# Bias pieces among the gates, paired groups at each new operand set, and x1 added by GpSimd, in a transformer block on one core

## The chip, the core and the metric

The kernel runs on one core of a Trainium2 chip. The core has five engines, each with its own instruction queue that is worked through in order: TensorE (PE, matrix products, weight loads shown apart as PEld), VectorE (DVE), ScalarE (ACT), GpSimd (POOL) and SyncE (SP, which here only issues transfers). 16 DMA engines move data; transfers that SP issues are on queue q1, those that GpSimd issues on q0. The metric is the device time of one execution in microseconds, as the median of several runs.

## The reference, cut to what matters

One block over x of shape (1, 2048, 1024), float32:

```
h      = rms_norm(x, norm1_g);   proj = h @ w_in          # 4608 columns: u, v | q, k, v | gates
y_a    = u * (w_s . layer_norm(v) + b_s)                  # gelu(u, v); chunks of 128 tokens
y_b    = neighbourhood_attention_2d(q, k, v, q_g, k_g, rpb)   # scores + bias from na_rpb, softmax
gates  = sigmoid(gate_pre + b_gate)
merged = gates[:, :D] * (y_a @ w_o_a) + gates[:, D:] * (y_b @ w_o_b)
x      = x + merged @ w_out                               # x1
h2     = rms_norm(x, norm2_g)
x      = x + square(relu(h2 @ w_ff1)) @ w_ff2             # up: 1024 -> 4096, down: 4096 -> 1024
```

## The kernel before, in words

Everything is computed transposed: features on the 128 partitions, tokens along the row, in two halves of 1024 tokens (h 0 and 1). Each float32 operand is split in a high and a low part (ACT casts the high part, DVE subtracts to get the low one), and a product is the sum of high x high, high x low and low x high.

The large products (the features of w_in, up and down) run in **groups**: a block of 256 output features by 1024 tokens, as seven products of half-sized operand sums in place of eight, in the order 1, 5, 6, 3, 7, 2, 4. A product is 12 matmuls of 128x128 by 128x512 for 4 operands (`seven`, matmul at L1537). It accumulates in a PSUM bank called z, x or y; after each product DVE or ACT **evacuates** the bank, that is adds or copies it to a tile in SBUF, and products that go on in the same bank wait for that. The stages of the program, with their start in the profiled execution: gates of half 0; the u features of half 1 (two groups, 243.8 us); gates of half 1 (eight groups, 278.0); values (450.5); keys and queries (to 880); attention; merge and output projection; then up of half 0 (16 groups, 1445.6), down of half 0 (1767.8), up of half 1 (2087.8) and down of half 1 (2408.2).

The operands of a product:

- `w_seven` (L1446): weights. SP loads two w_r tiles (L1458), GpSimd makes the sums w_s (L1464 to L1471), and `hilo` splits them (ACT cast L1418, DVE subtraction r_lo and t_lo L1422).
- `x_seven` (L1486): activations x_r and x_t, whose sums are made before and lie in DRAM (xf, hf, af). SP loads (L1497), ACT casts (L1505), DVE subtracts (L1509).
- `first_w` gives the values' and keys' weights their sums on GpSimd (L391 to L401, tiles w and t).

An up group (L1763 on) evacuates with a squared ReLU into tiles a_A to a_D, makes sums of them on GpSimd and stores them as af (L1816). **Down** (L1830 on) visits four output blocks j in turn, several times each, as af comes in: a visit is one group over up to four k. All seven evacuations of a visit are DVE additions to tile x1 (L1854), which is first loaded with the residual x1 from DRAM (L1439); the last visit's result is stored.

**Bias pieces.** Attention reads its biases from tables tb in DRAM. `bias_tables` (L1009 to L1077) makes them on GpSimd: memsets, a few loads with waits between (tbi L1021, sk L1024, tbx L1041), sums, and then 93 transfers tb<-tbi and tb<-tbx (L1056), all in one chain of 108 stages.

What sets the order: the kernel doesn't run its code in written order. `Plan` collects **steps** (one for each product) and **chains** of **stages** (a load, a cast, a subtraction, a sum, a store), each with an engine, a cost, a lead (how long before its first step it is due) and the buffers it takes and gives (51 buffers of one size). `Plan.run` then walks through the steps with planned times, and issues a stage behind a step if its engine is free in the plan and buffers are there, or when it is due; `put_off` can postpone one that is due. The result is only an order of instructions for each engine; on the chip an instruction starts when the engine reaches it and what it waits for has come.

Of the kernel before, what the change touches and what calls it, by code (L numbers as in the profile page):

```python
# [87 lines left out]
class Plan:  # L88
# [25 lines left out]
    def run(self):  # L114
# [156 lines left out]
class Block:  # L271
# [74 lines left out]
    def feat(self, h, xs, c0, row, act, dst, done, leads=(22, 14, 9)):  # L346
# [24 lines left out]
        ids = self.seven(w, xs, {1: copy(0, 0, True), 5: copy(1, 1, True), 6: copy(0, 1, False), 3: add(0, 1), 7: add(1, 1),  # L371
                                 2: add(0, 0), 4: (lambda bank: fin(1, 0, bank), 0, {"DVE": 0.7, "ACT": 0.7}, 0)})
        for i, p in ((0, 2), (1, 4)):
            def out(i=i):
                nc.sync.dma_start(dst(i), e[i][1].rearrange("p b t -> p (b t)"))
                self.give(e[i][0])
            done(i, (self.post(ids[p], [self.store(out, 1, 0)], 8), 1))
# [630 lines left out]
    def bias_tables(self, start, end):  # L1008
# [66 lines left out]
        c = self.plan.chain([Stage("POOL", 2.0, f, t, gv, 5 + 2.2 * (n - i), 0.0) for i, (f, t, gv) in enumerate(fs)], start=start)  # L1075
# [3 lines left out]
    def first_steps(self):  # L1079
# [31 lines left out]
        for c in range(2):  # L1111
            if c == 1:
                self.constants()
            self.first_w(0, 2 + c, len(plan.steps) + 6)

            def act(i, v):
                nc.scalar.activation(v, v, AF.Gelu)
            self.feat(1, xs, C_U + c * 256, lambda b: self.rows["in", 1, b], act,
                      lambda i, c=c: self.ut[(2 * c + i) * P : (2 * c + i + 1) * P, 1024:2048],
                      lambda i, d: self.ut_done[1].append(d))  # L1120
        for c in range(8):
# [3 lines left out]
            gates(1, xs, c)  # L1125
        start = len(plan.steps)
# [353 lines left out]
    def x_seven(self, src, after):  # L1480
# [4 lines left out]
        for name, (p0, p1) in self.X_PART.items():  # L1485
# [21 lines left out]
            def sub(name=name):  # L1507
# [4 lines left out]
                [Stage("SP", self.DMA * n / 2, load, 1, 0, 11, 3.0),  # L1512
                 Stage("ACT", 0.1 + 0.48 * n, cast, n - 1, 0, 6, 0.3), Stage("DVE", 0.1 + 0.58 * n, sub, 0, 0, 3, 0.2)],
# [3 lines left out]
    def seven(self, w, xs, evac, mid=None):  # L1517
# [4 lines left out]
        banks = {}  # L1522
        ids = {}
        for p in (1, 5, 6, 3, 7, 2, 4):
            bank = {5: "x", 3: "x", 2: "y"}.get(p, "z")
            (wn, wi), (xn, xi) = self.W_AT[p], self.X_AT[p]

            def mm(p=p, bank=bank, wn=wn, wi=wi, xn=xn, xi=xi):
                if p in (1, 5, 2):
                    banks[bank] = self.ps(bank, "mm" if p == 1 else "s")  # L1530
                out = banks[bank]
                at = lambda v, k: v[:, k] if wi is None else v[:, k, wi]
                for k in range(n):
                    a = [at(v, k) for v in w[0][wn][1]]
                    b = [v if xi is None else v[:, xi] for v in xs[k][0][xn][1]]
                    for j, (u, v) in enumerate(((0, 0), (0, 1), (1, 0))):
                        nc.tensor.matmul(out, a[u], b[v], start=(p in (1, 5, 2) and k == 0 and j == 0),  # L1537
                                         stop=(k == n - 1 and j == 2), skip_group_check=p in (6, 3, 7, 4))

            fn, take, costs, free = evac[p]  # L1540
            ids[p] = plan.step(3 * n * self.MM, mm, [w[1][wn]] + [x[1].get((xn, xi), x[1][xn]) for x in xs],
                               (lambda fn=fn, bank=bank: fn(banks[bank])), take, costs, free, ids.get({6: 1, 3: 5, 7: 6, 4: 7}.get(p)))
        w[2].first = ids[1]
# [74 lines left out]
    def out_proj(self, h, mgs):  # L1618
# [5 lines left out]
        for c in range(4):  # L1624
# [67 lines left out]
            def out(part, x, i, c=c):  # L1692
# [10 lines left out]
                ((k1, 1), (k2, 1)), start=step, due=24)  # L1703
# [60 lines left out]
    def up(self, h, mid):  # L1764
# [3 lines left out]
        xs = [self.x_seven(self.hf[h, c], (self.hf_done[h, c],)) for c in range(4)]  # L1768
        for c in range(self.NU):
            w = self.w_seven(w1, [0, 2, 4, 6], [1, 3, 5, 7], c * 256)  # L1770
            e = {}
# [24 lines left out]
            ids = self.seven(w, xs, mk())  # L1796
# [29 lines left out]
            if c in mid:  # L1826
                for f in mid[c]:
                    f()

# [102 lines left out]
```

## Time and profile before

| | us |
|---|---|
| median of 3 runs | 2734.75 |
| lowest and highest run | 2733.2, 2739.95 |
| the profiled execution, device time | 2740.49 |
| its span on the core | 2738.7 |
| PE busy (granted clock 0.967 on the mean) | 2553.1 |
| DVE, ACT, POOL busy | 1810.2, 1181.1, 1103.9 |

The profile is one execution. Its page gives busy times by engine; the other views give the same trace by stretch (busy time of each engine, the clock that TensorE was granted as a share of full speed, the DMA engines' busy share), by queue, by line, as a chain of what released what, and as lists of what an engine waited for. An engine's idle time matters only where the next matmul waits for it.

### The profile page before, as it was taken

The numbers are of one execution on the slowest core, as the hardware profiler recorded it, in microseconds if no ns is written. First come the engines' busy times: TensorE is split into PE (matmuls) and PEld (weight loads), VectorE is DVE, ScalarE is ACT, GpSimd is POOL, SyncE is SP. The second block draws the span as 40 slices with busy tenths as digits, with TensorE's granted clock in tenths as the row PEclk, the third lists the DMA queues.
The fourth block names the chain that finished last, engine by engine and source line by source line (L and its number), as shares of the span: only waits on it lengthen the run. The fifth ranks groups of instructions, "written<-read, shape, count | busy, mean of one in ns | idle before, by whom it ended". The sixth has DMA issues, their size and how long they took to land.

```text
span 2738.7 us, 34122 instructions
## 1 busy us (share of the span) xinstructions
PE 2553.1 (93%) x11832; PEld 2074.2 (76%) x11832; DVE 1810.2 (66%) x2588; ACT 1181.1 (43%) x1857; POOL 1103.9 (40%) x852
## 2 busy tenths in 40 slices
PE   7997999858898899999998999899998999979999
PEld 6776888647677777778886888778887888868887
DVE  5656657545888666563647566688777665677876
ACT  6555446334554555532324433433334343433341
POOL 3553541350000111132434677634343777743442
PEclk9998999979999999999999999999999999989999
DMA  5878658787768999996856444553436444374443
GB/s 169 288 222 263 212 186 287 187 214 219 238 179 210 295 309 310 322 365 231 277 197 199 143 146 156 203 202 135 169 131 228 153 157 154 137 273 140 149 148 112
DMA packets 401181, 569.20 MB, mean 208 GB/s; under 512 B 34093, under 2 KB 268756, under 8 KB 401008
## 3 DMA queue, kind: packets, MB, share of 16 engines
q1 hardware_dynamic: 388736, 553.45, 62.5%
q0 software_dynamic: 8128, 13.55, 2.1%
q8 instruction: 93, 1.52, 0.2%
q10 hardware_dynamic: 4144, 0.02, 0.1%
q14 instruction: 80, 0.66, 0.1%
HBM read 363.89 MB, written 202.98 MB: 207 GB/s over the span
## 4 chain that ended last, share of the span: by engine, by line
PE 69%; DMA 13%; DVE 9%; SPq 3%; ACT 2%; issue 2%; POOL 1%; ACTq 0%; DVEq 0%; POOLq 0%
PE z L1537 30%; PE x L1537 15%; PE fg L331 11%; PE y L1537 7%; DMA vw<-vs 2%; DMA x_t<-xf 2%; SPq L845 1%; PE z L713 1%; DMA x_r<-xf 1%; DVE x_r L1509 1%; PE fg L502 1%; PE pv L1292 1%; DMA y<-ya 1%; DMA bias<-tb 1%; PE x L713 1%
## 5 line engine op out<-in xcount | busy, mean ns | idle before, releaser
L1537 PE MATMUL z<-x_t,t_hi 128*128 128x512 f32 x1184 | 371.4, 395 | 32.5 <-DVE x L1854 25.8
L1464 POOL TENSOR_TENSOR w_s<-w_r 128x512 f32<-128x512 f32 (+3 forms) x87 | 150.3, 1727 | 524.4 <-DVE x L1854 226.3
L1422 DVE TENSOR_TENSOR r_lo<-w_r,r_hi 128x1024 fp32r<-128x1024 f32 (+3 forms) x174 | 254.2, 1463 | 83.1 <-ACT r_hi L1418 83.1
L1537 PEld LDWEIGHTS z<-x_t,t_hi 128*128 128x128 f32 x1184 | 224.2, 190 | 84.5 <-ACT t_hl L1418 16.8
L1167 POOL CAST q<-qn 128x256 fp32r<-128x256 f32 x128 | 49.3, 427 | 478.3 <-DMA qn<-qs 229.3
L1537 PE MATMUL z<-x_t,t_lo 128*128 128x512 f32 x592 | 233.9, 395 | 3.9 <-DVE t_lo L1422 3.9
L1537 PE MATMUL x<-x_r,t_hl 128*128 128x512 f32 x888 | 218.1, 393 | 8.1 <-DVE x_r L1509 5.8
L1418 ACT CAST r_hi<-w_r 128x1024 fp32r<-128x1024 f32 (+3 forms) x174 | 171.6, 988 | 119.5 <-PE z L1537 47.1
L1537 PEld LDWEIGHTS x<-x_r,t_hl 128*128 128x128 f32 x888 | 167.8, 189 | 45.6 <-DVE x_r L1509 7.5
L1505 ACT CAST x_r<-x_r 128x1024 fp32r<-128x1024 f32 x104 | 107.6, 1049 | 209.0 <-PE x L1537 152.2
L1537 PE MATMUL z<-x_r,r_hi 128*128 128x512 f32 x592 | 186.6, 397 | 5.5 <-DVE x_r L1509 5.5
L1537 PE MATMUL z<-x_t,r_hi 128*128 128x512 f32 x592 | 184.9, 394 | 5.9 <-DVE x L1854 3.4
L1537 PE MATMUL y<-x_r,r_hi 128*128 128x512 f32 x592 | 183.6, 391 | 0.0
L1537 PE MATMUL x<-x_r,r_hi 128*128 128x512 f32 x592 | 182.4, 389 | 0.0
L331 PE MATMUL fg<-y,w_hi 128*128 128x512 f32 x512 | 163.1, 400 | 7.9 <-DMA y<-ya 5.2
L1470 POOL TENSOR_TENSOR w_s<-w_r 128x512 f32<-128x512 f32 (+3 forms) x87 | 166.0, 1908 | 3.9
L1509 DVE TENSOR_TENSOR x_r<-x_r,x_r 128x1024 fp32r<-128x1024 f32 x104 | 147.4, 1436 | 20.7 <-ACT x_r L1505 20.7
L331 PE MATMUL fg<-mg,w_hi 128*128 128x512 f32 x512 | 157.7, 389 | 0.0
L1422 DVE TENSOR_TENSOR t_lo<-w_s,t_hi 128x1024 fp32r<-128x1024 f32 (+3 forms) x87 | 136.7, 1572 | 19.7 <-DMA af<-a_D 11.5
L1471 POOL TENSOR_TENSOR w_s<-w_r,w_s 128x512 f32<-128x512 f32 (+3 forms) x87 | 133.6, 1535 | 25.4 <-DVE t_lo L1422 7.8
L1854 DVE TENSOR_TENSOR x<-z,x 128x512 f32<-128x512 f32 x152 | 104.6, 688 | 59.2 <-PE z L1537 58.9
L1537 PEld LDWEIGHTS z<-x_r,r_hi 128*128 128x128 f32 x592 | 113.2, 192 | 29.6 <-DVE x_r L1509 5.8
(258 smaller groups left out, 5996.0 us busy)
## 6 DMA issues: line engine op xcount, KB each, us to landing
w_r<-in_w_ff_dram SPq DMA_DIRECT2D x116, 512.0 KB
x_r<-af SPq DMA_DIRECT2D x64, 512.0 KB
w_r<-in_w_in_dram SPq DMA_DIRECT2D x34, 512.0 KB
gt<-fe SPq DMA_DIRECT2D x32, 512.0 KB
x_r<-xf SPq DMA_DIRECT2D x32, 512.0 KB
qn<-qs SPq DMA_DIRECT2D x64, 256.0 KB
g<-gt SPq DMA_DIRECT2D x64, 256.0 KB
x<-x SPq DMA_DIRECT2D x32, 512.0 KB
```

The lines of the kernel that those rows point to most:

```text
L331: self.nc.tensor.matmul(out, w[p], x[q], start=(i == 0 and j == 0), stop=(i == n - 1 and j == 2))
L713: nc.tensor.matmul(out, a[u], b[v], start=(p in (1, 5, 2) and k == 0 and j == 0), stop=(k == 3 and j == 2), skip_group_check=p in (6, 3, 7 ...
L1167: nc.gpsimd.tensor_copy(e[0][1][:, cb].rearrange("p l (r c) -> p (l r) c", c=16), e[1][1].rearrange("p l (r f c) -> p f (l r) c", f=4, c=1 ...
L1418: nc.scalar.copy(e[name + "_"][1][0], e[name][1])
L1422: nc.vector.tensor_tensor(lo, e[name][1], hi.bitcast(F32), ALU.subtract)
L1464: nc.gpsimd.tensor_tensor(s23[:, :, 1], r1[:, :, 0], r1[:, :, 1], ALU.subtract)
L1470: nc.gpsimd.tensor_tensor(s23[:, :, 0], r1[:, :, 1], r1[:, :, 0], ALU.subtract)
L1471: nc.gpsimd.tensor_tensor(e["t4"][1], r2[:, :, 0], s23[:, :, 0], ALU.subtract)
L1505: nc.scalar.copy(hi, lo.bitcast(F32))
L1509: nc.vector.tensor_tensor(lo, lo.bitcast(F32), hi.bitcast(F32), ALU.subtract)
L1537: nc.tensor.matmul(out, a[u], b[v], start=(p in (1, 5, 2) and k == 0 and j == 0), stop=(k == n - 1 and j == 2), skip_group_check=p in (6, ...
L1854: nc.vector.tensor_tensor(v, bank, v, ALU.add)
```

## The change

1. The bias chain: its stages are planned on an engine of their own, "bias", with 3.7 us each (before: POOL, 2.0 us), and it may start before the u groups of half 1 (before: at the values). The instructions are still GpSimd's.
2. `feats` and `sevens`: groups can be run product by product together (1a 1b 5a 5b 6a 6b ...). This is done for the two u groups of half 1 (their constants' loads now come after them) and for groups 0 and 1 of each up, with shorter leads for the second group's weights and longer ones for x operands c = 1 to 3 (`early`).
3. Down: on the first visit of a block, products 1, 5, 6 and 4 are copied by ACT into a new tile "o", and 3, 7, 2 are added by DVE. x1 is loaded for later, and GpSimd adds it to the tile (128x1024) between two visits.
4. The planner: a stage with a lag (a store) is planned 2 us later and may be put off (`late`); a DVE or ACT stage may stand ahead of an evacuation if by the plan it ends 0.3 us and the evacuation's cost before the end of the next step (`room`). The hf sums' due time goes from 24 to 20.

```diff
-        self.lag = lag
+        self.lag, self.late = lag, 2.0 if eng == "SP" and lag else 0.0
...
+            t -= c.stages[k].late
-            if c.stages[k].eng not in ("ACT", "DVE") or i + 2 >= n or (c.first is not None and c.first <= i):
+            if (c.stages[k].eng not in ("ACT", "DVE") and not c.stages[k].late) or i + 2 >= n or (c.first is not None and c.first <= i):
...
+            room = self.steps[i + 1].cost - 0.3 if i + 1 < n else 0.0
-                    b = max(c.begin() if k else r, clock.get(st.eng, 0.0), now)
-                    if (b + st.cost > end + 0.1) if st.eng in ("DVE", "ACT") else b > end:
+                    b = max((c.begin() if k else r) + st.late, clock.get(st.eng, 0.0), now)
+                    if (b + st.cost > end + max(0.1, room - s.costs.get(st.eng, 0.0))) if st.eng in ("DVE", "ACT") else b > end:
...
-        c = self.plan.chain([Stage("POOL", 2.0, f, t, gv, 5 + 2.2 * (n - i), 0.0) for i, (f, t, gv) in enumerate(fs)], start=start)
+        c = self.plan.chain([Stage("bias", 3.7, f, t, gv, 8 + 3.9 * (n - i), 0.0) for i, (f, t, gv) in enumerate(fs)], start=start)
...
+        self.feats(xs, [first(0), first(1)])
+        self.constants()
...
-    def seven(self, w, xs, evac, mid=None):
+    def seven(self, w, xs, evac):
+        return self.sevens([(w, evac)], xs)[0]
+
+    def sevens(self, groups, xs):
...
+            for g, (w, evac) in enumerate(groups):
...
-                ((k1, 1), (k2, 1)), start=step, due=24)
+                ((k1, 1), (k2, 1)), start=step, due=20)
...
-        xs = [self.x_seven(self.hf[h, c], (self.hf_done[h, c],)) for c in range(4)]
+        xs = [self.x_seven(self.hf[h, c], (self.hf_done[h, c],), 1.3 * c) for c in range(4)]
...
+            w = self.w_seven(w1, [0, 2, 4, 6], [1, 3, 5, 7], c * 256, (16, 10, 6) if c == 1 else (22, 14, 9))
...
+        for cs in [(0, 1)] + [(c,) for c in range(2, self.NU)]:
...
-                    x1[m] = (e, plan.chain([self.load(e, "x1", [2, 512], self.x1[h, m], 5)], (self.x1_done[h, m],)))
...
+            new = j not in acc
+                    if first:
+                        e[m] = self.take([2, 512], F32, "o")
+                    nc.scalar.copy(e[m][1][:, b], bank)
+                return (f, int(first), {"ACT": 0.6}, 0)
...
+            put = copy if new else (lambda m, b, first: add(m, b))
-                             {1: add(0, 0), 5: add(1, 1), 6: add(0, 1), 3: add(0, 1), 7: add(1, 1), 2: add(0, 0), 4: add(1, 0)})
+                             {1: put(0, 0, True), 5: put(1, 1, True), 6: put(0, 1, False), 3: add(0, 1), 7: add(1, 1), 2: add(0, 0), 4: put(1, 0, False)})
...
+                            nc.gpsimd.tensor_tensor(e[m][1], e[m][1], x["x1"][1], ALU.add)
+                        ld = plan.chain([self.load(x, "x1", [2, 512], self.x1[h, i], 12)], (self.x1_done[h, i],))
+                        ch = plan.chain([Stage("POOL", 3.0, plus, 0, 1, 4, 0.3)], ((ld, 1),), start=ids[4])
```

The order of instructions shows the change at three places. (Lines of the changed file stand some 10 lower: L1056 is L1066, L1509 is L1520, L1854 is L1883.)

GpSimd, from the last gates to the bias tables, before: the last sums of the values' and keys' weights (tiles w and t), then the bias chain's first memset, its loads, and its pieces.

```order
L400 TENSOR_TENSOR t_3129<-w_3014 128x512
L401 TENSOR_TENSOR t_3152<-w_3055,t_3129 128x512
L1020 MEMSET tbi 120x96
L1021 DMA tbi<-in_na_rpb_dram 120x31
L1024 DMA sk<-tbi 1920x1x96
L1031 DMA tbi<-in_column_mask_dram 128x96
L1041 DMA tbx<-sk 16x15x32 x8
L1047 TENSOR_TENSOR tbx<-tbx,tbi 128x360
L1049 MEMSET tbi 128x528
L1050 COPY tbi<-tbx 128x192
L1056 DMA tb_83<-tbi 8x16x360
L1056 DMA tb_82<-tbx 8x16x192
```

GpSimd at the same place now, from a gate group's last weight sums (w_s) on:

```order
L1482 TENSOR_TENSOR w_s_3124<-w_r_3052,w_s_3077 128x512
L1066 DMA tb_82<-tbi 8x16x264
L1066 DMA tb_84<-tbi 8x16x288
L1066 DMA tb_83<-tbi 8x16x360
L401 TENSOR_TENSOR t_3202<-w_3083 128x512
L402 TENSOR_TENSOR w_3083<-w_3083,w_3103 128x512
L1066 DMA tb_82<-tbi 8x16x264
L410 TENSOR_TENSOR t_3202<-w_3083 128x512
L411 TENSOR_TENSOR t_3221<-w_3103,t_3202 128x512
L1066 DMA tb_84<-tbi 8x16x96
L1066 DMA tb_84<-tbx 8x16x192
L1066 DMA tb_83<-tbi 8x16x360
```

The chain's first memset now stands 71 rows above the last sum; its loads and 21 pieces are spread over the gates' sums, and the other 72 pieces follow that sum with no other GpSimd work between but the three instructions that make the second table's tbi.

SP where the first down begins, before: the af stores of up's 15th group (of 16), x1 loads (x<-x_95), operands x_t and x_r.

```order
L1816 DMA af<-a_A 128x1024
L1816 DMA af<-a_C 128x1024
L1816 DMA af<-a_B 128x1024
L1816 DMA af<-a_D 128x512
L1439 DMA x_14708<-x_95 128x1024
L1439 DMA x_14710<-x_95 128x1024
L1497 DMA x_t_14717<-af 128x1024
L1439 DMA x_14746<-x_95 128x1024
L1439 DMA x_14748<-x_95 128x1024
L1497 DMA x_r_14753<-af 128x1024
```

SP now, from 15 rows behind the 15th group's store of a_A on: the last stores of the 16th, operands, weights (w_r), and the first two x1 loads.

```order
L1835 DMA af<-a_B 128x1024
L1835 DMA af<-a_D 128x512
L1508 DMA x_t_14923<-af 128x512
L1508 DMA x_r_14936<-af 128x1024
L1508 DMA x_t_14952<-af 128x1024
L1508 DMA x_r_14968<-af 128x1024
L1469 DMA w_r_14984<-in_w_ff_dram 128x4x256
L1469 DMA w_r_14986<-in_w_ff_dram 128x4x256
L1508 DMA x_t_15006<-af 128x512
L1450 DMA x_15025<-x_95 128x1024
L1508 DMA x_t_15063<-af 128x1024
L1450 DMA x_15083<-x_95 128x1024
```

Before, the first x1 load stood 4 rows behind the 15th group's store of a_A, and the fourth 8; now the first stands 24 rows behind it, with eleven operands x_t and x_r and five weight tiles between, and the second two rows further.

DVE at the end of the first down, before: the last two visits' additions to x1 tiles, and the subtractions for the coming up (r_lo of a weight, x_r of its operands).

```order
L1854 TENSOR_TENSOR x_14748<-z,x_14748 128x512
L1854 TENSOR_TENSOR x_14874<-z,x_14874 128x512
L1854 TENSOR_TENSOR x_14876<-x,x_14876 128x512
L1422 TENSOR_TENSOR r_lo<-w_r_16823,r_hi 128x1024
L1509 TENSOR_TENSOR x_r_16945<-x_r_16945,x_r_16992 128x1024
L1509 TENSOR_TENSOR x_r_16929<-x_r_16929,x_r_16981 128x1024
L1509 TENSOR_TENSOR x_r_16912<-x_r_16912,x_r_16965 128x1024
L1509 TENSOR_TENSOR x_r_16914<-x_r_16914,x_r_16967 128x1024
L1854 TENSOR_TENSOR x_14874<-z,x_14874 128x512
L1854 TENSOR_TENSOR x_14874<-x,x_14874 128x512
L1854 TENSOR_TENSOR x_14876<-z,x_14876 128x512
```

The same now (tile o in place of x1's):

```order
L1883 TENSOR_TENSOR o<-y,o 128x512
L1520 TENSOR_TENSOR x_r_16929<-x_r_16929,x_r_16967 128x1024
L1883 TENSOR_TENSOR o<-z,o 128x512
L1520 TENSOR_TENSOR x_r_16961<-x_r_16961,x_r_17011 128x1024
L1883 TENSOR_TENSOR o<-z,o 128x512
L1883 TENSOR_TENSOR o<-x,o 128x512
L1433 TENSOR_TENSOR r_lo<-w_r_16839,r_hi 128x1024
L1520 TENSOR_TENSOR x_r_16980<-x_r_16980,x_r_17025 128x1024
L1883 TENSOR_TENSOR o<-z,o 128x512
L1883 TENSOR_TENSOR o<-x,o 128x512
```

Four x_r subtractions stood behind each other, ahead of the last five additions; now additions stand between them (three are in these rows, the fourth 11 rows above the first of them).

## Rows read from the trace of the kernel before

**Rows 1.** The page's first part: busy us (share of span) xinstructions, each engine.

```profile
PE 2553.1 (93%) x11832; PEld 2074.2 (76%) x11832; DVE 1810.2 (66%) x2588; ACT 1181.1 (43%) x1857; POOL 1103.9 (40%) x852
```

**Rows 2.** By stretch: us, busy PE, PEld, DVE, ACT, POOL, PEclk, DMA, GB/s.

```profile
243.80:278.00 34.20, 24.26 (x88) 18.59 (x87) 29.86 (x27) 20.04 (x27) 15.12 (x9) 0.85 0.76 248
278.00:450.50 172.50, 172.34 (x760) 141.97 (x759) 102.69 (x104) 78.69 (x107) 78.62 (x52) 1.00 0.63 219
450.50:489.60 39.10, 38.29 (x174) 31.02 (x173) 33.03 (x48) 28.59 (x39) 0.00 (x0) 1.00 0.73 241
489.60:623.40 133.80, 87.08 (x362) 71.03 (x361) 57.46 (x101) 42.27 (x58) 67.95 (x114) 0.81 0.80 208
1445.60:1501.00 55.40, 44.71 (x194) 35.86 (x192) 44.94 (x49) 24.36 (x37) 28.18 (x18) 0.94 0.60 192
1501.00:1767.80 266.80, 266.80 (x1180) 221.01 (x1179) 161.01 (x153) 106.44 (x157) 193.54 (x118) 1.00 0.44 151
1767.80:1803.00 35.20, 22.25 (x74) 16.22 (x73) 30.94 (x35) 16.92 (x24) 14.74 (x10) 0.81 0.80 295
1803.00:2087.80 284.80, 284.80 (x1257) 235.57 (x1256) 222.64 (x233) 108.03 (x123) 112.07 (x64) 1.00 0.48 163
2087.80:2114.50 26.70, 18.77 (x65) 13.84 (x65) 24.21 (x25) 12.49 (x17) 10.82 (x5) 0.87 0.76 250
2408.20:2443.60 35.40, 21.48 (x71) 15.62 (x70) 29.83 (x34) 16.91 (x24) 14.79 (x10) 0.76 0.81 290
```

**Rows 3.** PE's waits in 489.6-623.4, by releaser: us in total, times, longest.

```profile
PE x L713 <- ACT av L745: 18.8, 3, 8.9
PE z L713 <- DVE av L757: 17.8, 2, 9.8
```

**Rows 4.** DMA queues in 489.6-623.4: packets, MB, share of 16 engines.

```profile
q0 software_dynamic: 7910, 13.21, 41.2%
q1 hardware_dynamic: 15583, 14.51, 38.6%
```

**Rows 5.** PE's waits, one row each of 243.8-278, 1767.8-1803 and 2408.2-2443.6.

```profile
PE z L1537 <- DVE x_r L1509: 5.5, 1, 5.5
...
PE z L1537 <- DVE x L1854: 11.0, 3, 8.2
...
PE z L1537 <- DVE x L1854: 12.8, 4, 7.8
```

**Rows 6.** Timeline of SP's queue at the first down: start us, us, instruction.

```profile
1766.53 1.60 SPq L1439 DMA_DIRECT2D x<-x  x2
```

**Rows 7.** Timeline of DVE, 2088 to 2095.

```profile
2089.77 4.62 DVE L1509 TENSOR_TENSOR x_r<-x_r,x_r 128x1024 fp32r<-128x1024 f32 x4
```

**Rows 8.** Line L1056: count, ns min/median/max, first and last start.

```profile
L1056 POOL DMA_DIRECT2D tb<-tbi x72: 594/596/635, 514.4 to 622.2; - x72
L1056 POOL DMA_DIRECT2D tb<-tbx x21: 596/596/612, 515.0 to 622.8; - x21
```

**Rows 9.** Timeline of GpSimd, 414 to 424: its last sum before the tables.

```profile
420.74 2.15 POOL L401 TENSOR_TENSOR t<-w,t 128x512 f32<-128x512 f32 x1
```

**Rows 10.** DMA queues in 418-474.

```profile
q1 hardware_dynamic: 9267, 17.91, 92.0%
```

**Rows 11.** The chain of waits in 430-460: start us, us, what.

```profile
440.56 8.94 DMA x_t<-wf
```

**Rows 12.** Timeline of GpSimd, 423 to 520: in brackets the idle before, and its releaser.

```profile
505.93 4.54 POOL L1041 DMA_DIRECT2D tbx<-sk  x8 [9.00 <-DMA sk<-tbi]
```

**Rows 13.** Timeline of DVE, then of GpSimd, 1616 to 1624.

```profile
1618.08 2.31 DVE L1422 TENSOR_TENSOR r_lo<-w_r,r_hi 128x1024 fp32r<-128x1024 f32 x1
1622.64 1.34 DVE L1422 TENSOR_TENSOR r_lo<-w_r,r_hi 128x1024 fp32r<-128x1024 f32 x1 [2.26 <-ACT r_hi L1418]
...
1617.03 2.27 POOL L1804 TENSOR_TENSOR a_A<-a_D,a_A 128x512 f32<-128x512 f32 x1
1621.61 1.29 POOL L1471 TENSOR_TENSOR w_s<-w_r,w_s 128x512 f32<-128x512 f32 x1
```

More of the change, by code (lines that the diff above doesn't have):

```diff
@@ L369, in add, with end, out @@
             return (f, 0, {"DVE": 1.4, "ACT": 0.7}, 0)
[L371 to L377, printed above, removed]
+        def end(ids):
+            for i, p in ((0, 2), (1, 4)):
+                def out(i=i):
+                    nc.sync.dma_start(dst(i), e[i][1].rearrange("p b t -> p (b t)"))
+                    self.give(e[i][0])
+                done(i, (self.post(ids[p], [self.store(out, 1, 0)], 8), 1))
+        return w, {1: copy(0, 0, True), 5: copy(1, 1, True), 6: copy(0, 1, False), 3: add(0, 1), 7: add(1, 1),
+                   2: add(0, 0), 4: (lambda bank: fin(1, 0, bank), 0, {"DVE": 0.7, "ACT": 0.7}, 0)}, end
     def sums(self, e, r1, r2, t23, t4, kind):
@@ L1124, in first_steps @@
                 self.first_w(1, c // 2, i)
-            gates(1, xs, c)
-        start = len(plan.steps)
+            self.feats(xs, [gates(1, c)])
         for p, f in ((0, self.values), (1, self.queries)):
@@ L1515, in x_seven @@
         return e, out
-    def seven(self, w, xs, evac, mid=None):
+    def seven(self, w, xs, evac):
+        return self.sevens([(w, evac)], xs)[0]
+    def sevens(self, groups, xs):
         nc, plan = self.nc, self.plan
         n = len(xs)
-        banks = {}
-        ids = {}
+        banks = [{} for _ in groups]
+        ids = [{} for _ in groups]
         for p in (1, 5, 6, 3, 7, 2, 4):
[L1525 to L1543, printed above, removed]
@@ new lines, in sevens, with mm @@
+            for g, (w, evac) in enumerate(groups):
+                bank = {5: "x", 3: "x", 2: "y"}.get(p, "z")
+                (wn, wi), (xn, xi) = self.W_AT[p], self.X_AT[p]
+                def mm(p=p, bank=bank, wn=wn, wi=wi, xn=xn, xi=xi, w=w, banks=banks[g]):
+                    if p in (1, 5, 2):
+                        banks[bank] = self.ps(bank, "mm" if p == 1 else "s")
+                    out = banks[bank]
+                    at = lambda v, k: v[:, k] if wi is None else v[:, k, wi]
+                    for k in range(n):
+                        a = [at(v, k) for v in w[0][wn][1]]
+                        b = [v if xi is None else v[:, xi] for v in xs[k][0][xn][1]]
+                        for j, (u, v) in enumerate(((0, 0), (0, 1), (1, 0))):
+                            nc.tensor.matmul(out, a[u], b[v], start=(p in (1, 5, 2) and k == 0 and j == 0),
+                                             stop=(k == n - 1 and j == 2), skip_group_check=p in (6, 3, 7, 4))
+                fn, take, costs, free = evac[p]
+                ids[g][p] = plan.step(3 * n * self.MM, mm, [w[1][wn]] + [x[1].get((xn, xi), x[1][xn]) for x in xs],
+                                      (lambda fn=fn, bank=bank, banks=banks[g]: fn(banks[bank])), take, costs, free,
+                                      ids[g].get({6: 1, 3: 5, 7: 6, 4: 7}.get(p)))
@@ L1544, in seven @@
+        for (w, _), i in zip(groups, ids):
+            w[2].first = i[1]
         return ids
@@ L1825, in up @@
             self.af_done[h, c] = (k4, 6)
-            if c in mid:
-                for f in mid[c]:
+        for cs in [(0, 1)] + [(c,) for c in range(2, self.NU)]:
+            es = [{} for _ in cs]
+            for c, e, ids in zip(cs, es, self.sevens([group(c, e) for c, e in zip(cs, es)], xs)):
+                after(c, e, ids)
+            for c in cs:
+                for f in mid.get(c, ()):
                     f()
```

76 lines of the change are left out of this document (42 added, 34 removed).

## The prediction

> **What bounds the kernel now.** The page's first part says that TensorE (PE) is busy 2553.1 us, 93% of the span [rows 1], so time is to be found only where PE idles or runs at a lower clock. The table by stage shows where. In the long stages PE never stops: 1180 matmuls in 266.8 us and 1257 in 284.8 us, at a granted clock of 1.00 (the 2.4 GHz level) [rows 2]. That is 0.226 us for a matmul, 2.7 us for a product of twelve; PE idle there is nil, so nothing can be won there, only lost. Against that rate six stretches lose time [rows 2], each length less matmuls x 0.226: the keys' and values' stretch 489.6-623.4, 133.8 - 362 x 0.226 = **52.0**; start of the u groups, 34.2 - 88 x 0.226 = **14.3**; first up, 55.4 - 43.8 = **11.6**; second up, 26.7 - 14.7 = **12.0**; the two downs' starts, 35.2 - 16.7 = **18.5** and 35.4 - 16.0 = **19.4**. Together 128 us, and the change touches all six. Part of each is clock: 0.76 to 0.94 there, a mix of the 1.2 and 2.4 GHz levels after PE had idled [rows 2].
>
> What ends the waits, from the waits of PE. In the long stretch they are evacuations of the values (18.8 us, 17.8 us) [rows 3], which themselves wait for tiles that a store or a load holds: the bias pieces on queue q0 take 41.2% of the DMA engines, more than everything on q1 (38.6%) [rows 4], and 40 us earlier, without q0, PE was fully fed (450.5-489.6) [rows 2]. At the u groups it is one x_r operand (5.5 us), at both downs the first evacuation (11.0 and 12.8 us) [rows 5], which adds to a tile that the x1 load has yet to fill: those loads stand in SP's queue among the visit's operands [rows 6]. At the second up four x_r subtractions, 4.62 us in one block, stand between the last visit's evacuations [rows 7].
>
> **The change, part by part.**
>
> A. Bias pieces. The same 93 transfers are issued, from 514.4 to 622.8 us: 1.17 us a piece [rows 8]. The planner now gives each 3.7 us and lets them start before the u groups. But only its order is carried out, not its pace: on GpSimd 21 pieces stand among the gates' sums, and behind the last sum 72 follow each other with nothing between. That sum ran at 420.74 [rows 9]. So I expect 72 x 1.17 = 84 us of pieces from 423 to about 507, not a thin spread. q0's work was 0.412 x 133.8 = 55 us of all engines [rows 2, 4]; the 72 pieces have 79% of the bytes, so 43 us. Where they now fall, q1 alone is at 92.0% [rows 10], and the chain of waits there is DMA (x_t<-wf, 8.94 us) [rows 11], with PE following at once: no slack. Up to 474 us the loads need 0.92 x 51 = 47 us and the pieces 43 x 51/84 = 26: 73 in 51, so 22 us late. Then 18 us of pieces are left beside the values, at the old rate of 52.0/133.8 = 0.39 us lost for each: 7. Lost after: 29 of 52, so **-22**. Bounds: 0 (the same loss at another place) and -52 (all hidden); I take the middle, since the bytes don't shrink and a fifth of them do move into a stage with 37% of DMA time free (278-450.5, share 0.63) [rows 2].
>
> What each DMA engine does with two queues the page doesn't show. The Trainium skill (DMA: Bandwidth & Descriptors, section Queues, rings and completion order) says that it goes round robin between the queues that have work, a packet at a time. By that the pieces would get all they ask, 43 in 84 us or half of the engines, and the loads would be done some 40 us late, not 22; A would be -12 and the time 2683. No row shows both queues with a backlog at once, so it stays at that.
>
> The prologue of the pieces moves with them, into the gates' sums. It makes GpSimd wait for its own transfers, 9.00 us at the worst place [rows 12], and now w_s sums and their ACT and DVE stages are queued behind. GpSimd is busy 78.6 of 172.5 us there [rows 2], so I put it at nothing, up to +9 if a product waits.
>
> B. The u groups of half 1 run 1a 1b 5a 5b and so on: each new x operand serves two products, 5.4 us, before the next is due. Nothing is removed. The idle time goes down by what the operands gain: half, **-7** (bounds +2, for a second set of weights that is needed sooner, and -12). The constants' loads now stand behind.
>
> C and D. The first two groups of each up likewise: 11.6 and 12.0 us. In D the order also shows the x_r subtractions one at a time between the adds, so the block of 4.62 us [rows 7] goes. **-8** (0 to -12) and **-7** (0 to -12); what is late next is the weights of the second group, due six steps sooner.
>
> E. Down. Of the first visit's seven evacuations four become ACT copies into a fresh tile and wait for no load; the x1 loads fall some 20 rows later on SP, behind the operands. The waits named, 11.0 and 12.8 us, end [rows 5]; what is next is the operand loads themselves (DMA share 0.80 [rows 2]), which the later stores of af don't speed. I take half of 18.5 + 19.4: **-18** (0 to -30). Added: 16 GpSimd sums of 128x1024, 2 x 2.27 us each by the half-sized one [rows 13], 73 us on an engine busy 112.1 of 284.8 in a down [rows 2], between visits; nothing on the path if they are done a round of visits later. ACT has room as well (108.0 of 284.8).
>
> F. The planner's new rules (stores later; a subtraction may stand ahead of an evacuation) and hf's due time: 0, +-10. The order puts one subtraction between two evacuations where three stood behind the last; DVE is busy 161.0 of 266.8 and 222.6 of 284.8 us [rows 2].
>
> Sum: -22 - 7 - 8 - 7 - 18 = **-62**. The profiled execution took 2740.5 us (span 2738.7), so 2678.5; the runs' median is 5.7 lower: **2673**.
>
> **The rivals.**
>
> 1. The burst costs what it saves: A is 0, and the time 2695, up to 2722 if B to E bring half. For it: [rows 10, 11]. Against: a fifth of the bytes is out of the way, and the pieces end 115 us sooner.
> 2. The spread works: values' operands arrive in time, A is -52, the time 2643. For it: before, the stretch without q0 ran at full rate. Against: 72 pieces in a row at a full queue. That the change doesn't do what its words say is part of the main case.
> 3. GpSimd's sums hold DVE up. A subtraction that began at 1618.08 beside a GpSimd sum took 2.31 us and ended 1.09 us after that sum did; the next, at 1622.64, ended 1.08 us after its neighbour [rows 13]. So a subtraction seems to wait out the GpSimd operation, and an evacuation queued behind it waits too. Sums of 2.27 us were absorbed (PE 284.8 of 284.8); one of 4.5 us would cost the 2.3 that it is longer, 16 times: 36, the time 2709. The Trainium skill (SBUF — State Buffer, section SBUF: two separate sides) gives it as a rule: a VectorE operation with two SBUF inputs and a GpSimd one that reads SBUF exclude each other for the whole instruction. The trace agrees with these two.
> 4. Slower: with the new rule a subtraction of 1.1 to 2.3 us delays the evacuation behind it, and PE waits for the bank, in the long stages where it waited for nothing. Some 600 products x 0.2 us = 122, the time 2795; it decides from 0.1 us a product, which eats the 62. For it: DVE is 78% busy in down. Against: a product lasts 2.7 us, and there are several banks.
> 5. Nothing moves: the stage starts are bound by the loads, whose bytes are the same (share 0.76 to 0.81 [rows 2]), and the burst is a wash: 2735.
>
> **How the numbers follow.** Chances: main case (2655 to 2692) 0.50; burst 0.17; all hidden 0.12; GpSimd holds DVE 0.09; slower 0.08; nothing 0.04. The range 2640 to 2722 takes in the first four but for their tails. A measurement of this kernel tells 0.3%, 8 us. Faster by more 0.86, within 0.06, slower 0.08.
>
> **What would show it.** A: L1066 issues back to back from about 423 to 507, and PE idle of some 20 us near 450 that ends with x_t or x_r operands; no stretch like 489.6-623.4 behind it. B: the wait for x_r gone from the u groups. C, D: under 6 us lost at each up. E: no wait of PE for an addition at the downs' starts; x1 loads behind the operands. F: PE still without idle in the long stages, against rival 4. Wrong would make it: pieces that GpSimd issues slowly by themselves (rival 2), a PE idle in the gates behind the prologue, or subtractions of over 4 us in down beside the new sums (rival 3).

## The result, and the profile after

The changed kernel takes 2703.8 us (median of 4 runs, 2696.3 to 2704.7) against 2734.6 us: a ratio of 0.9878, 95% interval 0.9855 to 0.9900. It is faster by 31 us where 62 were forecast. The time lies inside the range (2640 to 2722), but above the main case's 2655 to 2692, which had a chance of 0.50.

The page of the changed kernel, first part (busy time, share of the span of 2702.8 us):

```profile
PE 2540.5 (94%) x11832; PEld 2057.9 (76%) x11832; DVE 1783.4 (66%) x2556; ACT 1199.4 (44%) x1889; POOL 1100.1 (41%) x868
```

The table by stretch of the changed kernel, for the stretches of [rows 2]; columns as there. The cuts are not at exactly the same products: the first row holds 12 matmuls more than in [rows 2], the third and fourth together 7 more:

```profile
239.40:263.80 24.40, 22.97 (x100) 17.87 (x99) 22.91 (x17) 18.68 (x25) 10.16 (x6) 1.00 1.06 335
263.80:442.90 179.10, 173.41 (x750) 141.70 (x749) 105.43 (x113) 74.28 (x101) 106.96 (x108) 0.98 0.73 230
442.90:496.10 53.20, 41.78 (x173) 33.25 (x171) 32.50 (x44) 30.80 (x39) 28.09 (x47) 0.87 0.96 310
496.10:584.80 88.70, 79.58 (x370) 66.17 (x370) 62.22 (x106) 44.95 (x62) 4.22 (x8) 0.94 0.71 210
1400.20:1447.40 47.20, 42.20 (x196) 34.81 (x194) 42.03 (x49) 26.46 (x40) 24.69 (x15) 0.97 0.60 213
1447.40:1734.30 286.90, 272.40 (x1178) 221.21 (x1177) 148.52 (x158) 107.13 (x160) 175.07 (x116) 0.99 0.43 143
1734.30:1762.60 28.30, 21.41 (x74) 16.31 (x73) 25.30 (x26) 15.15 (x24) 14.55 (x10) 0.82 0.88 312
1762.60:2048.70 286.10, 285.87 (x1258) 235.39 (x1256) 226.88 (x224) 113.24 (x135) 129.77 (x76) 1.00 0.53 169
2048.70:2067.20 18.50, 15.04 (x65) 11.82 (x65) 18.13 (x20) 11.66 (x13) 0.02 (x1) 1.00 0.99 342
2379.90:2406.40 26.50, 20.50 (x71) 15.39 (x70) 24.83 (x25) 14.95 (x23) 15.78 (x10) 0.82 0.86 309
```

Every stretch that was to become shorter did: the start of the u groups from 34 to 24 us, values and first keys from 176 to 142 at the same products (third and fourth row together), first up 55 to 47, second up 27 to 18, the downs' starts 35 to 28 and 35 to 26. The first row of [rows 2] holds the first u group and little more; the second ran in the row behind it, before the gates. Over both u groups together, 170 matmuls, the time fell from 52.3 to 41.0 us. But the long stretch of up, in which PE had no idle time, grew from 266.8 to 286.9 us [rows 2], and that of the second up grew by 19 as well. The waits of PE in 1447.4-1734.3 name one new releaser (us in total, times, longest):

```profile
PE z L1552 <- ACT a_A L1799: 14.1, 11, 1.5
```

Eleven waits, one in nearly every up group, for ACT's copy of product 1. PE's busy time is also longer there (272.4 us for 1178 matmuls, 266.8 for 1180 before); the two make up the 20 us.

The bias pieces ran as a burst, as forecast. GpSimd's timeline at its last sum (start us, us), and line L1066 over the whole run:

```profile
409.68 0.61 POOL L1066 DMA_DIRECT2D tb<-tbi  x1
410.32 1.66 POOL L410 TENSOR_TENSOR t<-w 128x512 f32<-128x512 f32 x1
412.05 1.62 POOL L411 TENSOR_TENSOR t<-w,t 128x512 f32<-128x512 f32 x1
413.62 0.61 POOL L1066 DMA_DIRECT2D tb<-tbi  x1
...
L1066 POOL DMA_DIRECT2D tb<-tbi x72: 594/596/637, 337.2 to 499.5; - x72
L1066 POOL DMA_DIRECT2D tb<-tbx x21: 596/596/624, 340.8 to 501.5; - x21
```

From 413.6 to 501.5 us 72 pieces follow each other (forecast: 423 to 507), with some waits for earlier transfers between, the longest 10.8 us. Beside them PE waits for the values' evacuations (waits of PE in 442.9-584.8, which answer to [rows 3]):

```profile
PE z L723 <- ACT vg L755: 11.0, 2, 9.0
PE z L723 <- DVE av L767: 9.5, 2, 9.1
```

20.5 us in place of the 36.6 in the two rows before: less, not gone. What the two long ones wait for stands on the evacuating engine. ACT near 456 us, then SP and DVE near 500:

```profile
456.30 0.62 ACT L1516 CAST x_t<-x_t 128x512 fp32r<-128x512 f32 x1 [4.16 <-DMA x_t<-wf]
456.82 0.58 ACT L755 COPY vg<-z 128x512 f32<-128x512 f32 x1
...
481.56 14.69 SPq L855 DMA_DIRECT2D vs<-av  x16
496.67 1.44 SPq L802 DMA_DIRECT2D uT<-ut  x2
...
501.78 0.69 DVE L827 TENSOR_TENSOR y<-mix,spc 128x512 f32<-128x512 f32 x1 [8.86 <-DMA uT<-ut]
504.49 0.68 DVE L767 TENSOR_TENSOR av<-z,av 128x512 f32<-128x512 f32 x1
```

The copy vg<-z stands on ACT behind a cast that waits 4.16 us for its operand's load. The evacuation av<-z stands on DVE behind an addition that waits 8.86 us for the load uT, and SP issues that load only after 16 stores, which hold its queue for 14.69 us.

### The profile page after: what moved, and what is told of

Same layout as the page of the kernel before. It is cut to its first block, busy times and chain, and to the rows that moved or that the text cites. A ratio compares the mean times of both kernels' runs of the same rounds, so it can differ in the third digit from the quotient of the medians.

```text
span 2702.8 us, 34022 instructions
## 1 busy us (share of the span) xinstructions
PE 2540.5 (94%) x11832; PEld 2057.9 (76%) x11832; DVE 1783.4 (66%) x2556; ACT 1199.4 (44%) x1889; POOL 1100.1 (41%) x868
## 4 chain that ended last, share of the span: by engine, by line
PE 49%; DMA 12%; POOL 11%; issue 11%; DVE 11%; ACT 3%; SPq 2%; POOLq 0%; DVEq 0%; ACTq 0%
PE z L1552 17%; PE fg L333 11%; PE x L1552 8%; PE y L1552 4%; PE z L723 3%; POOL w_s L1475 2%; POOL w_s L1482 2%; POOL w_r L1476 2%; DMA vw<-vs 1%; DMA qn<-qs 1%; DMA x_r<-xf 1%; PE x L723 1%; POOL w_s L1481 1%; DMA x_r<-wf 1%; POOL a_D L1829 1%
## 5 line engine op out<-in xcount | busy, mean ns | idle before, releaser
L1433 DVE TENSOR_TENSOR r_lo<-w_r,r_hi 128x1024 fp32r<-128x1024 f32 (+3 forms) x174 | 244.0, 1404 | 124.7 <-ACT r_hi L1429 118.7
L1475 POOL TENSOR_TENSOR w_s<-w_r 128x512 f32<-128x512 f32 (+3 forms) x87 | 141.5, 1627 | 430.6 <-DVE t_lo L1433 235.9
L1520 DVE TENSOR_TENSOR x_r<-x_r,x_r 128x1024 fp32r<-128x1024 f32 x104 | 163.9, 1587 | 30.9 <-ACT x_r L1516 30.8
L1482 POOL TENSOR_TENSOR w_s<-w_r,w_s 128x512 f32<-128x512 f32 (+3 forms) x87 | 150.5, 1730 | 29.9 <-PE z L1552 10.5
L1516 ACT CAST x_t<-x_t 128x1024 fp32r<-128x1024 f32 (+1 forms) x104 | 85.5, 837 | 169.8 <-PE z L1552 118.4
L1433 DVE TENSOR_TENSOR t_lo<-w_s,t_hi 128x1024 fp32r<-128x1024 f32 (+3 forms) x87 | 113.3, 1303 | 52.2 <-ACT t_hi L1429 51.1
L1476 POOL TENSOR_TENSOR w_r<-w_r,w_r 128x512 f32<-128x512 f32 (+3 forms) x87 | 134.3, 1544 | 10.4 <-DMA w_r<-in_w_in_dram 2.2
L1552 PEld LDWEIGHTS z<-x_t,r_hi 128*128 128x128 f32 x592 | 111.0, 189 | 35.0 <-DVE o L1883 10.4
```

Of the source, the lines that this page charges most:

```text
L1433: nc.vector.tensor_tensor(lo, e[name][1], hi.bitcast(F32), ALU.subtract)
L1475: nc.gpsimd.tensor_tensor(s23[:, :, 1], r1[:, :, 0], r1[:, :, 1], ALU.subtract)
L1476: nc.gpsimd.tensor_tensor(r1[:, :, 1], r1[:, :, 1], r2[:, :, 1], ALU.add)
L1482: nc.gpsimd.tensor_tensor(e["t4"][1], r2[:, :, 0], s23[:, :, 0], ALU.subtract)
L1516: nc.scalar.copy(hi, lo.bitcast(F32))
L1520: nc.vector.tensor_tensor(lo, lo.bitcast(F32), hi.bitcast(F32), ALU.subtract)
```

## The experiments

All times are medians of four runs; the kernel before took 2734.0, 2736.3 and 2733.4 us on the chips of the three series. The stretches given below are cut at the same products in each trace, the long stretches of the ups within a few matmuls.

**1. Without the room rule.**

```diff
-                    if (b + st.cost > end + max(0.1, room - s.costs.get(st.eng, 0.0))) if st.eng in ("DVE", "ACT") else b > end:
+                    if (b + st.cost > end + 0.1) if st.eng in ("DVE", "ACT") else b > end:
```

> The changed kernel with the planner's room rule taken back (a DVE or ACT stage may end at most 0.1 us behind the step, as before); all else as changed. In the changed kernel's trace PE waits 1.37 us in each up group for ACT's copy of product 1 (a_A), and the long stretches of the two ups became 20.3 and 18.9 us longer. Theory R (the room rule puts the subtractions r_lo and t_lo ahead of the additions a_B and a_A, which then come late, and everything behind them): the 1.37 us waits go, both ups shrink by 19 us each, median about 2665 (2658 to 2676). Rival L (the wait comes from the later stores, which move r_hi's cast behind the last a_B on ACT): the waits stay, 2700 to 2708.

Measured: 2655.1 us, ratio 0.9712 (0.9690 to 0.9734). 49 us less than the changed kernel, more than the 39 of both ups. Theory R holds for the ups: no wait of PE is left in either long stretch; the first is 268.7 us long (266.8 before the change), the second 293.8. The other 10 us came back in the gates (179.1 to 170.6) and the queries (200.2 to 187.6), while the first row's stretch of the u groups lost 4.5 (24.4 to 28.9): there the rule had helped.

The timelines show how it does it. DVE and then ACT in one up group of the changed kernel, with the PE wait behind:

```profile
1506.90 1.48 DVE L1433 TENSOR_TENSOR t_lo<-w_s,t_hi 128x1024 fp32r<-128x1024 f32 x1 [1.64 <-ACT t_hi L1429]
1508.30 0.68 DVE L1805 TENSOR_TENSOR a_A<-y,a_A 128x512 f32<-128x512 f32 x1
1509.01 1.07 DVE L1806 SCALAR_TENSOR_TENSOR a_A<-a_A,rs_row 128x512 f32<-128x512 f32 x1
1510.00 1.78 DVE L1433 TENSOR_TENSOR t_hl<-w_s,t_hl 128x512 fp32r<-128x512 f32 x1
1511.71 0.68 DVE L1791 SCALAR_TENSOR_TENSOR a_B<-z,rs_row 128x512 f32<-128x512 f32 x1
...
1512.42 0.63 ACT L1792 ACTIVATE a_B<-a_B 128x512 f32<-128x512 f32 x1 [1.67 <-DVE a_B L1791]
1512.96 1.03 ACT L1429 CAST r_hi<-w_r 128x1024 fp32r<-128x1024 f32 x1
1513.89 0.58 ACT L1799 COPY a_A<-z 128x512 f32<-128x512 f32 x1
...
1514.52 0.73 PE L1552 MATMUL z<-x_t,t_hi 128*128 128x512 f32 x2 [1.47 <-ACT a_A L1799]
```

The subtraction t_lo waits 1.64 us for its cast, and the evacuation a_A<-y, which needs nothing from it, stands behind. From there on everything comes late: t_hl, then the evacuation a_B<-z, then on ACT a_B and a cast, and only then the copy a_A that frees bank z for product 6. The same place without the rule, DVE and then ACT:

```profile
1499.82 0.69 DVE L1805 TENSOR_TENSOR a_A<-y,a_A 128x512 f32<-128x512 f32 x1 [0.17 <-PE y L1552]
1500.54 0.81 DVE L1806 SCALAR_TENSOR_TENSOR a_A<-a_A,rs_row 128x512 f32<-128x512 f32 x1
1502.56 0.69 DVE L1433 TENSOR_TENSOR t_hl<-w_s,t_hl 128x512 fp32r<-128x512 f32 x1 [1.21 <-ACT t_hl L1429]
1503.17 0.68 DVE L1791 SCALAR_TENSOR_TENSOR a_B<-z,rs_row 128x512 f32<-128x512 f32 x1
1503.77 1.72 DVE L1433 TENSOR_TENSOR t_lo<-w_s,t_hi 128x1024 fp32r<-128x1024 f32 x1
...
1504.42 1.04 ACT L1429 CAST r_hi<-w_r 128x1024 fp32r<-128x1024 f32 x1
1505.36 0.57 ACT L1799 COPY a_A<-z 128x512 f32<-128x512 f32 x1
1507.98 0.59 ACT L1799 COPY a_B<-x 128x512 f32<-128x512 f32 x1 [2.04 <-PE x L1552]
```

Here DVE waits for PE (0.17 us behind product 2) and t_lo comes after the evacuations; a_A is copied 2 us before product 5 ends.

**2. Without the later stores.**

```diff
-        self.lag, self.late = lag, 2.0 if eng == "SP" and lag else 0.0
+        self.lag, self.late = lag, 0.0
```

> The changed kernel with late set to 0, so that stores are planned as before and not put off; the room rule stays. Theory R: the waits of 1.4 us in each up group stay, as r_lo and t_lo still stand ahead of a_B and a_A; 2700 to 2708. Rival L: they go, about 2665.

Measured: 2816.6 us, ratio 1.0307 (1.0288 to 1.0327): neither. The waits did stay, but they doubled, 2.7 us in place of 1.4 (12 waits, 31.9 us, in the first up), and the gates grew by 15 us. So the two rules work on each other: with the later stores the room rule costs 49 us (experiment 1), without them 144 (against experiment 5).

**3. Bias pieces issued by SP, at the planned places.**

```diff
-                    g.dma_start(self.tb[ct][kind][:, rq, :, k0 * w : (k0 + r1 - r0) * w],
+                    nc.sync.dma_start(self.tb[ct][kind][:, rq, :, k0 * w : (k0 + r1 - r0) * w],
```

> The changed kernel with the 93 bias pieces issued by SP in place of GpSimd, at the same places of the plan: SP has loads and stores between them all the way to the queries, so here the spread that is planned is also carried out, and the burst of 72 pieces from 423 to 501 us is gone. Theory B (the burst costs what is left of the loss around the values, some 25 us: two waits of 9 us and a lower clock): the waits of 8.97 us near 448 and 9.12 us near 496 shrink to under 3 us and 12 to 25 us are won, 2680 to 2692. Rival S (the same bytes cost the same wherever they stand beside the values and keys, or SP's queue is held by the pieces): no gain, 2698 to 2715.

Measured: 2694.3 us, ratio 0.9856 (0.9837 to 0.9875): 9.5 us less than the changed kernel, just under the 12 expected and beyond the other theory; but the two ratios' intervals overlap, so the size is not certain. Values and first keys (142 us) became 134, the gates 6 us shorter; the rest of the keys gave 9 back. The two waits of 9 us shrank to 3.5 and 1.9.

**4. 2.0 us planned for a piece in place of 3.7, with the same leads**: 47 pieces among the gates.

```diff
-        c = self.plan.chain([Stage("bias", 3.7, f, t, gv, 8 + 3.9 * (n - i), 0.0) for i, (f, t, gv) in enumerate(fs)], start=start)
+        c = self.plan.chain([Stage("bias", 2.0, f, t, gv, 8 + 3.9 * (n - i), 0.0) for i, (f, t, gv) in enumerate(fs)], start=start)
```

> The changed kernel with 2.0 us in place of 3.7 planned for a bias piece, leads unchanged: 47 pieces stand among the gates' sums on GpSimd (21 before), 46 in the burst behind the last sum. Theory B: half the burst, some 10 us less lost at the values, but more DMA time taken from the gates (share now 0.7 or so), up to 5 us lost there: 2694 to 2702. Rival S: no difference, 2700 to 2708; if the pieces hold the weights' sums up on GpSimd, the gates grow by over 10 us and it is slower, 2708 to 2720.

Measured: 2704.1 us, ratio 0.9891 (0.9873 to 0.9908), no difference, for two reasons that cancel: values and first keys took 129 us (142 before the edit) and the queries 7 us less, but the gates 203 us, 24 more.

**5. Neither planner rule** (edits 1 and 2 together).

> The changed kernel with both planner rules taken back: no room, and late set to 0. Taking back late alone cost 113 us, taking back room alone won 49. Theory I (late is worth something only against the harm of room, since by delaying loads and casts it loosens the order that room tightens): without room, late makes no difference, 2645 to 2670. Rival G (late is a gain of its own in all stages): the loss is seen again, over 2690.

Measured: 2672.3 us, ratio 0.9772 (0.9756 to 0.9788). This is parts A to E of the change by themselves, and they win 64 us. (With them is hf's due time, which no run takes apart.) Against 2655.1 with the later stores, those are worth 17 us: just outside theory I, far from rival G. Values and first keys took 144 us in place of 139; the rest is spread, with 6 us in the first gates, 3 in the u groups and 7 in attention.

**6. Without the room rule, and the pieces by SP** (edits 1 and 3).

> The changed kernel without the room rule, and with the 93 bias pieces issued by SP at the planned places. With room this won 9.5 us. Theory B (the burst's cost is separate from the rest): 2640 to 2650. Rival S (the gain was a gates' matter of the room rule): 2652 to 2662.

Measured: 2647.9 us, ratio 0.9681 (0.9664 to 0.9698), the fastest of all, 2% under the changed kernel. Line L1066 now issues from 329.7 to 701.6 us, and the waits of PE at the values and first keys (437.1-560.6) are

```profile
PE z L723 <- DVE av L767: 3.8, 5, 1.5
PE z L723 <- ACT vg L755: 2.5, 2, 1.3
```

Its gain over experiment 1 is 7 us, with intervals that overlap and in another series; in the traces values and first keys fell from 139 to 124 us and 13 us of that were given back in keys and queries.

**7. Without the room rule, with the former down** (the function `down` of the kernel before put back).

> The changed kernel without the room rule, and with the former down: all evacuations are additions to a loaded x1 tile, no GpSimd sums. Theory E (the wait for x1 is what the starts of down lost): the first of each down is 6 to 9 us longer again, the rest of each 0 to 3 shorter, 2663 to 2672. Rival K (the operands' loads set the starts anyway): within 4 us, 2651 to 2659.

Measured: 2661.3 us, ratio 0.9731 (0.9707 to 0.9754): 6 us more than experiment 1, between the two theories and not clear of the noise (the intervals overlap). The starts of down were 2.6 and 3.9 us longer (32.1 and 30.3), not 6 to 9. Over both downs to their ends the difference is only 2.7, since the rest of the second one took 290.8 us in place of 295.4. That gap is not the new down's by itself: with it, experiments 5 and 8 have 290.5 and 290.4.

**8. Without the room rule, groups one by one.**

```diff
-        self.feats(xs, [first(0), first(1)])
+        self.feats(xs, [first(0)])
         self.constants()
+        self.feats(xs, [first(1)])
...
-        for cs in [(0, 1)] + [(c,) for c in range(2, self.NU)]:
+        for cs in [(c,) for c in range(self.NU)]:
```

(and the former leads of weights and operands). 

> The changed kernel without the room rule, and with all groups run one by one, as before, with the former leads. Theory P (the pairing gives the operands time): the u groups 5 us, first up 6, second up 8 longer again, 2670 to 2678. Rival Q (the gain there comes from the planner's later stores and hf's due time): under 6 us together, 2652 to 2661.

Measured: 2665.4 us, ratio 0.9748 (0.9734 to 0.9763), 10 us more than experiment 1, between theory P's range (2670 to 2678) and the rival's. The two u groups together were 7.3 us longer and the second up 8.2, as theory P has it. The first up's start was 3.9 longer, but the whole first up only 1.8 (320.1 against 318.3). Other stages moved too, in both directions: half 1's gates were 2.8 us longer, the first gates 2.5 and the second down's rest 5.0 shorter.

Why the first up gains so little shows in PE's waits at its start, in the changed kernel:

```profile
PE rs_T L1752 <- DVE ms L1739: 3.8, 1, 3.8
PE rs_T L1752 <- DVE rs_b L1747: 0.7, 1, 0.7
```

With pairs PE comes sooner to the products that turn the norm's scale (rs_T), and waits there for DVE; before, no wait of that stage names rs_T. In experiment 1 these two waits are 5.0 and 2.1 us, and in the 4.5 us behind them the granted clock is 0.50.

**9. Without the room rule, with the former bias chain** (planned on GpSimd with 2.0 us, from the values on).

> The changed kernel without the room rule, and with the bias chain as before (planned on GpSimd, 2.0 us a piece, from the values on). Theory A (the earlier pieces are the largest gain, some 27 to 40 us around values and keys): 2682 to 2698, with values and keys together back near 230 us from 190. Rival V (the gain there comes from the later stores of the values, not from the bias): under 12 us, 2655 to 2667.

Measured: 2678.0 us, ratio 0.9793 (0.9758 to 0.9828): the new chain is worth 23 us here, give or take some 10 by the intervals, less than theory A expected. Values and keys were 217 us, not 230, against 190 with the new chain. The later stores had already won a part: alone in the kernel before they bring these stages to 216 us (experiment 11).

**10 to 12. One part alone, in the kernel before**: the room rule; the later stores; the new bias chain with its earlier start.

```diff
+            room = self.steps[i + 1].cost - 0.3 if i + 1 < n else 0.0
-                    if (b + st.cost > end + 0.1) if st.eng in ("DVE", "ACT") else b > end:
+                    if (b + st.cost > end + max(0.1, room - s.costs.get(st.eng, 0.0))) if st.eng in ("DVE", "ACT") else b > end:
```

> The kernel before with the room rule alone added. Theory R: PE waits in each up group for ACT's copy of product 1, as in the changed kernel but without the later stores that halve it, 2.7 us and more a group: up's long stretches 35 to 60 us longer each, gates up to 22, in all 2800 to 2860. Rival N (the rule harms only together with another part of the change): 2725 to 2745.

> The kernel before with the later, postponable stores alone added. Without room, taking it back cost 17 us, at the values' start. Theory V (the later stores clear SP's queue for the values' operands, whatever the bias does): 10 to 25 us won, 2710 to 2725. Rival T (only where the bias pieces collide with that start, as in the changed kernel): within 6 us, 2728 to 2741.

> The kernel before with the new bias chain alone. Theory A: values and keys 35 to 45 us shorter, the values' first stretch 10 to 28 us longer, gates within 6: 2700 to 2722. Rival V (without the later stores the values' start pays all of it back): 2725 to 2745.

| kernel before with | us | ratio (95%) |
|---|---|---|
| room alone | 2854.5 | 1.0442 (1.0418 to 1.0467) |
| later stores alone | 2705.3 | 0.9892 (0.9865 to 0.9919) |
| new bias chain alone | 2698.8 | 0.9862 (0.9829 to 0.9894) |

Room alone costs 121 us. Its waits of PE in the second up's long stretch, and DVE in one group of the first up:

```profile
PE z L1538 <- ACT a_A L1783: 37.4, 14, 2.7
...
1549.73 0.68 DVE L1789 TENSOR_TENSOR a_A<-y,a_A 128x512 f32<-128x512 f32 x1
1550.44 1.07 DVE L1790 SCALAR_TENSOR_TENSOR a_A<-a_A,rs_row 128x512 f32<-128x512 f32 x1
1551.44 1.79 DVE L1423 TENSOR_TENSOR t_hl<-w_s,t_hl 128x512 fp32r<-128x512 f32 x1
1553.15 2.30 DVE L1423 TENSOR_TENSOR r_lo<-w_r,r_hi 128x1024 fp32r<-128x1024 f32 x1
1555.38 0.68 DVE L1775 SCALAR_TENSOR_TENSOR a_B<-z,rs_row 128x512 f32<-128x512 f32 x1
```

Two subtractions, 4.1 us, stand ahead of a_B; in the changed kernel's rows above it is one. So the later stores, with which r_lo's cast stands behind a_B, take away the second. Experiment 2, without them, has r_lo ahead of a_B again, 2.30 us. The later stores alone win 28 us, theory V and a little more, 16 of it at values and keys and 6.5 at the starts of down. The bias chain alone wins 35, a little more than theory A's range: the values' first stretch grew by 24 us, the rest of values and keys fell by 59.

## Why the prediction was right, and where its sum failed

**The sum of A to E held**: -62 forecast, 64 won without the two planner rules (experiment 5). That it came so close is partly luck, since the terms are not what was forecast and don't add up: taken back one at a time beside the later stores, A, the pairing of B to D, and E cost 23, 10 and 6 us, 39 together. And that the time lies in the range, though above the main case, owes something to luck too: 2704 is where rival 1 (the burst costs what it saves, 2695 to 2722) put it, and the cause was the planner rules. Term by term, in us:

| term | forecast | stretch before to after | alone or undone |
|---|---|---|---|
| A bias | -22 | values and keys 232 to 196 | -35 alone (12), -23 beside the later stores (9) |
| B u groups | -7 | both groups 52.3 to 41.0 | -7.3 (8) |
| C first up | -8 | 55.4 to 47.2 | -3.9, -1.8 over the whole up (8) |
| D second up | -7 | 26.7 to 18.5 | -8.2 (8) |
| E downs' starts | -18 | 35.2 to 28.3, 35.4 to 26.5 | -6.5, -2.7 over the whole downs (7) |
| F planner rules | 0, +-10 | both ups +39, gates +7 | -17 later stores (5), +49 room (1) |

**F is the term that was mis-sized**: 0 +-10 was written, +31 measured (2703.8 with both rules, 2672.3 with neither). The step that failed is "the order puts one subtraction between two evacuations where three stood behind the last": that is so, but the subtraction waits there for its cast, and the evacuation behind it waits with it (1.64 us in the rows of experiment 1). DVE's idle time, from which F was argued, says nothing about this: DVE is busy only 148.5 of 286.9 us there. The prediction had the mechanism as rival 4 (a subtraction delays the evacuation, PE waits for the bank), with 122 us and a chance of 0.08; alone in the kernel before the rule costs 121. The two numbers agree by chance: it was worked out as 0.2 us on each of 600 products, with DVE 78% busy in down named for it, where the runs show one wait of up to 2.9 us in nearly every up group and next to nothing in the downs. In the changed kernel it came in part, 49 us, since the later stores remove one of two subtractions. That those stores are a gain by themselves, 28 us in the kernel before, was in no term.

**A was right in its mechanism and place**: no thin spread but 72 pieces in a row up to 501 us, loads and pieces together at a DMA share of 0.96, two waits of 9 us, near 448 and near 496 us, and little loss behind. The first hangs on a late operand load as forecast (x_t, by way of ACT's cast); the second hangs on SP's queue, which the prediction didn't name. Rival 1 (the burst is a wash) falls by the 35 and 23 us, rival 2 (all hidden) by the two waits; a real spread (6) takes these away. The prediction's second sum for A (-12) is farther off. The rule behind it isn't tested by that: from 427 to 502 us q0 took 39.6% of the DMA engines' time and q1 56.6%, but GpSimd waited between its pieces, so q0 had no steady backlog. The bytes moved to the gates cost little at this pace: without the room rule half 1's gates take 154.7 us behind the u groups, pieces and prologue in them (1), and 154.6 before. They cost 24 us when half of the pieces stand there (4).

**B and D** came out near their halves. **C** was mis-sized: its stretch became 8 us shorter, but over the whole first up the pairing is worth 1.8, since PE only comes sooner to the wait for the norm's scale (8), which the prediction had nowhere.

**E had the right size for the stretches and the wrong owner.** They became 15.8 us shorter, 18 were forecast. But the later stores alone already shortened them by 6.5 us (11: to 32.8 and 31.1), and the copies in place of x1 by 6.5 (7). What was late next was not the operand loads, as the prediction had it: in the changed kernel's first down PE waits for evacuations still, at most 2.8 us for ACT's copy and 3.4 for an addition.

**Rival 3** (GpSimd's sums hold DVE) is there and costs nothing that shows in the changed kernel. In the changed kernel's second down (DVE, then GpSimd)

```profile
2429.10 3.42 DVE L1433 TENSOR_TENSOR r_lo<-w_r,r_hi 128x1024 fp32r<-128x1024 f32 x1
2432.44 1.21 DVE L1520 TENSOR_TENSOR x_t<-x_t,x_t 128x1024 fp32r<-128x1024 f32 x1
2433.57 0.68 DVE L1883 TENSOR_TENSOR o<-x,o 128x512 f32<-128x512 f32 x1
...
2425.25 6.18 POOL L1898 TENSOR_TENSOR o<-o,x 128x1024 f32<-128x1024 f32 x2
```

a subtraction beside the second of two sums takes 3.42 us and ends 1.09 after it (2425.25 + 6.18 = 2431.43; 2432.52), as in [rows 13]; the next one, without such a neighbour, takes 1.21. But PE stays busy 285.87 of 286.10 us in that stage of the first down and waits 0.5 us in the second's, and the 16 sums take 2.85 us each in the median, not the 4.5 worked out from a row of 2.27. That row was the dear one: [rows 13] has a sum of the same size at 1.29 us, and twice that is nearer.

**What stays open.** Why the gates take 24 us more with 47 pieces among their sums (queue held on GpSimd, or DMA time) was not told apart. Nor was why room helps the u groups by some 4 us. That late stores win at the values' start by clearing SP's queue is only argued: the runs show where they win, and the rows at 481 to 505 us that stores in SP's queue can hold an evacuation there, but no run ties the two together. The due time of the hf sums was never taken back by itself.

## What to carry to other kernels

An evacuation is due when PE's next product in its bank is; a preparing operation may go ahead of it only if all that it waits for is done by then, not merely if the engine has time: one subtraction waiting 1.6 us for its cast cost 1.4 us in nearly every group of a stage that had no idle time. The two long waits at the values are of the same kind. Test the rules of a scheduler one by one and together: of two here one won 28 us and one lost 121, and each changed what the other did. A chain that is planned with a slow pace runs at that pace only on an engine that has other work between; issued by a queue that stays busy, the same pieces were a spread and not a burst.

## What the runs showed of the hardware

The price of a GpSimd operation is no constant: sums of 128x512 took from 1.29 to 2.27 us in the same stage [rows 13], those of 128x1024 from 2.39 to 3.45. A DVE subtraction with both inputs in SBUF ended about 1.09 us after the GpSimd operation that it overlapped, in three places, whether it took 1.3, 2.3 or 3.4 us ([rows 13], and the rows of the second down above). The Trainium skill (SBUF — State Buffer, section SBUF: two separate sides) states that a VectorE operation with two SBUF inputs and a GpSimd operation that reads SBUF exclude each other for a whole instruction. These three places agree.
